# 160 gathered tokens instead of 192, second-table groups of 8 blocks, and x normalised once: one step of a hybrid decoder with product-key experts

## The chip, the cores and the metric

The kernel runs on one core of one Trainium2 chip. The metric is the device time of one execution in microseconds (us). A time of a kernel is the median of several executions; a profile is of one execution more, with a time of its own.

## The reference

One decoder layer for 512 prompt tokens and 8 x 4 sample tokens, 544 in all, of width 2048. A combined projection, a gated MLP and an RWKV-7 recurrence make the hidden state `h`; none of that is touched. What follows is the expert part:

```
def peer_ffn(xn, ...):                        # xn = rms_norm(h) * norm2_g
    q = xn @ w_q                              # 8 heads, 2 halves of 128
    s = q . sub_keys                          # 128 scores per head and half
    top 16 of each half -> 256 sums -> top 16 experts, gates = softmax of their scores
    act = gelu(u_tab[expert] . xn)            # 16384 experts, a row of 2048 each
    out = sum over 8 * 16 experts of gate * act * v_tab[expert]
y = rms_norm(h + out) * final_g
```

All is float32. Each token thus needs 128 rows of `u_tab` and 128 rows of `v_tab`, two tables of 134 MB each.

## The kernel before

`front` computes the projection, the two head groups and part of the output projection. `back` (from line 610) does the rest, and the diff touches it alone. Matrix products are split in three: a weight tile is loaded (`wr`), rounded to a short form on ScalarE (`wh`, line 661) and its remainder is taken on VectorE (`wl`, line 662); the product is `wh*xh + wh*xl + wl*xh`. Each table tile holds 1024 columns of 128 and serves 24 matmuls.

The expert part treats the tokens in two ways. The first `TD` = 352 tokens use **whole tables**: for each of 128 blocks of 128 experts, `activations` (line 763) multiplies the block of `u_tab` with all 352 tokens (48 matmuls, line 675), and `products` (line 1062) multiplies blocks of `v_tab` with the coefficients (line 1071). The coefficients are the Gelu of the first times `G`, a table of gates that is zero where a token has not chosen an expert. `G` is built in groups of `GT` = 32 tokens (`NG` = 11 groups, lines 1016 to 1032) and stored in HBM (`Gd`). The last `TG` = 192 tokens use **gathers**: waves of 32 tokens, each with 64 steps in which GpSimd's indirect DMA (line 807) fetches 128 rows of 8 KB and VectorE makes one pass over them, a dot product with x for `u_tab` (line 819) or a weighted sum for `v_tab` (line 838). `ROWS` = 3 buffers hold the rows. `finish` sums a wave's results with a few matmuls (line 862), adds h, normalises and stores.

Order of the stages in `back`: the output projection's second half, with h, its square sum and x = h times `norm2_g` (not yet divided by the norm; `xh`, `xl` for the first 416 tokens, `th`, `tl` for the last 128, whose queries come out transposed); the query product with the top-k of the last two token tiles beside it; then the top-k and `decode` of the other three tiles, each step with one `early` first-table block beside it, whose activations go to HBM (`Cd`); then `G`, with an early block per group; then the main loop over 128 blocks. 52 early blocks, the odd ones 1 to 103, are done before the main loop. There each is loaded from `Cd`, the others are computed. For every block GpSimd multiplies by `G` (line 1055, from `gl`, loaded for four blocks at a time), ScalarE rounds the coefficients to `ch` (line 1058) and GpSimd takes the remainder `cl` (line 1059). After each `GB` = 4 blocks come 8 calls of `products`. Each fills two PSUM tiles of 12 matmuls; six tiles exist. VectorE adds each tile to `y` (line 1079), which is `last`. `cc` has `GB + 2` = 6 slots for `ch` and `cl`.

Because x is not yet divided by its norm, every first-table block is multiplied by `rs2` on VectorE as it leaves PSUM (line 768); the Gelu follows on ScalarE (line 769). `last` is the multiplication, and `gathers` makes the next fetch and the next pass wait for it:

```python
        work[0] += n if steps else 0
        while nstep[0] < min(STEPS, int(work[0])):
            ...
            steps[0].send(after)
```

A step is due at fixed places: one per early block, and in the main loop `PACE * left` steps are spread with weight 6 on a computed first-table block and 4 on a call of `products`, 1480 in all.

Engines run their instructions in order. Within an engine the order comes from a scheduler with priorities: table splits are drawn ahead (by 300 in the main loop, 1500 before it), the eviction of a block by 60. Queues: SP issues all loads, GpSimd the stores to HBM and the gathers.

Of the kernel before, what the change touches and what calls it, by code (L numbers as in the profile page):

```python
# [11 lines left out]
OP = mybir.AluOpType  # L12
# [575 lines left out]

TG = 192
TD = TC - TG  # L590
# [7 lines left out]
GT = 32  # L598
GB = 4
STEPS = (64 + ROWS - 1) * NW  # L600
# [9 lines left out]
def back(tc, I, O, SC):  # L610
# [35 lines left out]
    res = pool(es, "res")  # L646
    bv = res.tile([128, ntile, 8, 16], F32, name="bv")
    e1 = res.tile([128, ntile, 8, 16], F32, name="e1")
    e2 = res.tile([128, ntile, 8, 16], F32, name="e2")
    idx = [res.tile([128, 32], U32, name=f"idx{w}") for w in range(NW)]  # L650
# [36 lines left out]

    rsp = pool(es, "rsp")
    rs2 = rsp.tile([128, TC], F32, name="rs2")
    ms = rsp.tile([TT, 1], F32, name="ms")  # L690
    with ExitStack() as s1:
# [4 lines left out]
        yp = pool(s1, "yp")  # L696
        xh = x2.tile([128, KT, TQ], F32R, name="xh2")
        xl = x2.tile([128, KT, TQ], F32R, name="xl2")
        xt = pool(xts, "xt", side="right")
# [60 lines left out]

    cp = pool(es, "cp", 3)
# [25 lines left out]
    gp, rows, po = [], [], []  # L787

    def gather_steps(w):
        c = WAVES[w]  # L790
        t, r0 = divmod(c, 128)
        rw = slice(r0, r0 + 32)
        xrow, acc = rows
        ef = gp[0].tile([128, 128], F32, name="ef")
        V.scalar_tensor_tensor(ef[rw], f2(e1[rw, t]), 128.0, f2(e2[rw, t]), op0=OP.mult, op1=OP.add)
        for j in range(4):
            js = slice(j * 32, j * 32 + 32)
            V.tensor_copy(idx[w][js], ef[rw, js])
            V.tensor_copy(gts[w][js], f2(bv[rw, t])[:, js])
        msw = gp[0].tile([128, 1], F32, name="msw", bufs=2)  # L800
# [88 lines left out]
    def open_gathers():  # L889
# [4 lines left out]
        next(steps[0])  # L894

    with ExitStack() as s1:
        tk = pool(s1, "tk", 2)
# [58 lines left out]
        for h in range(8):  # L956
# [34 lines left out]
            topk(sc[:, 1], 4, h)  # L991
            topk(sc[:, 0], 3, h)
        early(3)
        decode(4)
        decode(3)
        open_gathers()
        for t in range(3):
            for h in range(8):
                early(1)
                topk(sc0[:, h, t], t, h)  # L1000
            early(ED)
            decode(t)


    NG = TD // GT
    NE = -(-TD // 128)
    with ExitStack() as s1:
# [24 lines left out]
        early(EARLY)  # L1032


    yp = pool(es, "y")
    yT = yp.tile([128, KT, TD], F32, name="y")
    with ExitStack() as s1:
        vp = pool(s1, "vp")
        cc = pool(s1, "cc", GB + 2)
        po.append(pool(s1, "po", 6, space=PSUM))  # L1040
        r4 = lambda t: t.rearrange("p (g t) -> p g t", t=GT)
        NGR = 128 // GB
        gl, cs, ss = {}, {}, []

        def coefficients(b):
            g, i = divmod(b, GB)
            if i == 0:
                gl[g] = vp.tile([128, NG, GB, GT], F32, name="gl", bufs=2)
                S.dma_start(gl[g], SC["G"][:, :, b:b + GB].rearrange("g p b t -> p g b t"))
# [5 lines left out]
            G.tensor_mul(r4(ac), r4(ac), gl[g][:, :, i])  # L1055
            ch = cc.tile([128, TD], F32R, name="ch")
            cl = cc.tile([128, TD], F32R, name="cl")
            A.copy(ch, ac)
            G.tensor_sub(cl, ac, ch)  # L1059
            cs[b] = ch, cl  # L1060

        def products(g, m2):
            ws = split(wp, I["vT"][g, m2], 300)
            ps = [po[0].tile([128, 512], F32, name="o") for j in range(2)]
            for i0, i1 in ((0, GB - 1), (GB - 1, GB)):
                for j in range(2):
                    for i in range(i0, i1):
                        hi, lo = (w[:, (j * GB + i) * 128:(j * GB + i) * 128 + 128] for w in ws)
                        ch, cl = cs[g * GB + i]
                        for n, (a, x_) in enumerate(((hi, ch), (hi, cl), (lo, ch))):  # L1070
                            T.matmul(ps[j][:, :TD], a, x_, start=i + n == 0,  # L1071
                                     stop=i == GB - 1 and n == 2)
            for j in range(2):
                m = 2 * m2 + j
                prev = yT[:, m]
                if g == 0:
                    prev = vp.tile([128, TD], F32, name="hr")
                    S.dma_start(prev, SC["hT"][m][:, :TD])
                last = V.tensor_add(yT[:, m], ps[j][:, :TD], prev)  # L1079
                if g == NGR - 1:  # L1080
                    if m == 0:
                        A.activation(ss[0], yT[:, m], AF.Square)
                    else:
                        sq = cp.tile([128, TD], F32, name="ac")
                        A.activation(sq, yT[:, m], AF.Square)
                        G.tensor_add(ss[0], ss[0], sq)
                    A.activation(yT[:, m], yT[:, m], AF.Copy, scale=P("fg", m))
            return last


        left = STEPS - work[0]
        total = VW * 8 * NGR + UW * (128 - EARLY)
        for b in range(128 + 1):
            if b == 128:
                ss.append(vp.tile([128, TD], F32, name="hr"))
            if b < 128:
                coefficients(b)
                if b > GB and b not in firsts:
                    gathers(PACE * left * UW / total, last)
            if b and b % GB == 0:  # L1100
                for m2 in range(KT // 2):
                    last = products(b // GB - 1, m2)
# [50 lines left out]
def layout(inp):  # L1153
# [11 lines left out]
    for n in ("w0", "a0", "k_k", "k_a", "r_k", "gn_g", "gn_b"):  # L1165
# [27 lines left out]
    out["vT"] = np.ascontiguousarray(  # L1193
        out["v_tab"].reshape(128 // GB, GB, 128, 8, 2, 128).transpose(0, 3, 2, 4, 1, 5)
    ).reshape(128 // GB, 8, 128, 2 * GB * 128)
    return out
# [27 lines left out]
```

## Time and profile before

| | us |
|---|---|
| median of 3 runs | 4056.84 (4054.25 to 4058.28) |
| the profiled execution | 4046.83 |
| its span, first to last instruction | 4044.7 |
| TensorE / VectorE / ScalarE / GpSimd busy | 3632.6 / 3084.6 / 1425.5 / 1282.9 |

The mean granted clock of TensorE is 0.958 of full speed. The time of an execution is a little longer than its span. Busy shares are of the whole span; matmuls overlap, so a busy TensorE is not one at its peak. The stages lie in this order: `front` to about 1062 us, the output projection to 1285, the query product to 1472, early blocks and top-k to 1866, `G` to about 2043, the main loop to about 4025.

### The profile page before, as it was taken

To read this page: it belongs to the slowest core of one execution; us is meant where nothing else is said; L and a number is where in the kernel's file an instruction comes from. 1 tells how busy PE (TensorE), PEld (TensorE's weight loads), DVE (VectorE), ACT (ScalarE), POOL (GpSimd) and SP (SyncE) were. 2 spreads that over 40 slices of the span, in tenths; PEclk is the share of its full clock that TensorE was granted. 3 is DMA by queue.
4 is the path that set the end of the run, shared out by engine and by line. 5 is a ranking of instruction groups with operands and counts; after the bars stand their busy time and mean duration, and the time that the engine had idled before them with its cause. 6 is when DMAs were issued, how large, how long until landed. Compare 5 with 4: busy or idle time off the path is not lost.

```text
span 4044.7 us, 65633 instructions
## 1 busy us (share of the span) xinstructions
PE 3632.6 (90%) x25519; PEld 3413.5 (84%) x25519; DVE 3084.6 (76%) x5034; ACT 1425.5 (35%) x2501; POOL 1282.9 (32%) x1190
## 2 busy tenths in 40 slices
PE   8999999999999998889988888888988888898997
PEld 8888888887898997889888778887978788888997
DVE  4566666666645579999957888888898888888995
ACT  4244444444333232227942222222222222223233
POOL 1212222222143002221134443444434443444453
PEclk9999999999999999999999989999999998999998
DMA  4211111112554236667677898889889888998983
GB/s 156 102 62 56 58 59 57 59 57 78 178 170 120 75 115 234 235 225 260 252 242 287 311 341 310 318 310 341 317 326 325 317 322 305 333 331 311 358 332 123
DMA packets 252822, 886.53 MB, mean 219 GB/s; under 512 B 26920, under 2 KB 84008, under 8 KB 200480
## 3 DMA queue, kind: packets, MB, share of 16 engines
q1 hardware_dynamic: 184672, 423.77, 31.5%
q0 software_dynamic: 67840, 458.57, 30.3%
q8 instruction: 201, 3.29, 0.3%
q14 instruction: 109, 0.89, 0.1%
HBM read 823.47 MB, written 58.76 MB: 218 GB/s over the span
## 4 chain that ended last, share of the span: by engine, by line
PE 47%; DVE 16%; issue 15%; DMA 12%; POOL 8%; ACT 1%; SPq 0%; DVEq 0%; POOLq 0%; ACTq 0%
PE g L171 10%; PE o L1071 9%; PE g L675 9%; DMA row<-in_v_tab,idx 4%; PE q L970 4%; DVE wl L662 4%; DMA row<-in_u_tab,idx 3%; POOL row L807 3%; PE i L419 2%; DVE row L819 2%; DMA wr<-in_vT 2%; PE g L573 2%; POOL ac L1055 2%; POOL cl L1059 2%; DMA wr<-in_uT 1%
## 5 line engine op out<-in xcount | busy, mean ns | idle before, releaser
L661 ACT CAST wh<-wr 128x1024 fp32r<-128x1024 f32 x560 | 585.7, 1049 | 1441.4 <-PE o L1071 540.5
L662 DVE TENSOR_TENSOR wl<-wr,wh 128x1024 fp32r<-128x1024 f32 x560 | 730.3, 1308 | 205.2 <-ACT wh L661 200.4
L1071 PE MATMUL o<-ch,wh 128*128 128x352 f32 x2048 | 688.3, 343 | 190.1 <-DVE y L1079 146.8
L675 PE MATMUL g<-xh,wh 128*128 128x352 f32 x2048 | 678.3, 331 | 70.0 <-DVE ac L768 59.0
L1071 PE MATMUL o<-cl,wh 128*128 128x352 f32 x2048 | 695.0, 340 | 41.7 <-POOL cl L1059 41.7
L1071 PE MATMUL o<-ch,wl 128*128 128x352 f32 x2048 | 687.2, 337 | 0.7 <-DVE wl L662 0.7
L675 PE MATMUL g<-xh,wl 128*128 128x352 f32 x2048 | 672.9, 329 | 3.5 <-DVE wl L662 3.5
L675 PE MATMUL g<-xl,wh 128*128 128x352 f32 x2048 | 671.8, 328 | 0.0
L1071 PEld LDWEIGHTS o<-ch,wh 128*128 128x128 f32 x2048 | 407.5, 200 | 218.1 <-DVE y L1079 80.5
L819 DVE SCALAR_TENSOR_TENSOR row<-row,xrow 128x2048 f32<-128x2048 f32 x192 | 457.2, 2382 | 92.1 <-DMA row<-in_u_tab,idx 90.8
L838 DVE SCALAR_TENSOR_TENSOR acc<-row,dots,acc 128x2048 f32<-128x2048 f32 x186 | 458.8, 2467 | 63.7 <-DMA row<-in_v_tab,idx 61.6
L807 POOL DMA_INDIRECT row<-in_u_tab,idx x192 | 291.0, 1516 | 618.1 <-DVE y L1079 259.1
L675 PEld LDWEIGHTS g<-xh,wh 128*128 128x128 f32 x2048 | 391.4, 191 | 81.8 <-issue 40.9
L1071 PEld LDWEIGHTS o<-cl,wh 128*128 128x128 f32 x2048 | 411.2, 201 | 49.2 <-POOL cl L1059 49.0
L807 POOL DMA_INDIRECT row<-in_v_tab,idx x192 | 264.7, 1379 | 572.1 <-DVE y L1079 341.6
L1071 PEld LDWEIGHTS o<-ch,wl 128*128 128x128 f32 x2048 | 409.8, 200 | 1.0 <-DVE wl L662 1.0
L675 PEld LDWEIGHTS g<-xh,wl 128*128 128x128 f32 x2048 | 392.0, 191 | 5.6 <-DVE wl L662 5.4
L675 PEld LDWEIGHTS g<-xl,wh 128*128 128x128 f32 x2048 | 393.0, 192 | 1.0 <-issue 1.0
L171 PE MATMUL g<-xh,wh 128*128 128x276 f32 x1248 | 379.3, 304 | 9.6 <-ACT xh L113 9.6
L171 PE MATMUL g<-xl,wh 128*128 128x276 f32 x1248 | 375.9, 301 | 0.2 <-DVE xl L114 0.2
L171 PE MATMUL g<-xh,wl 128*128 128x276 f32 x1248 | 374.6, 300 | 0.0
L1079 DVE TENSOR_TENSOR y<-o,y 128x352 f32<-128x352 f32 x496 | 238.7, 513 | 36.0 <-PE o L1071 36.0
(636 smaller groups left out, 6378.6 us busy)
## 6 DMA issues: line engine op xcount, KB each, us to landing
wr<-in_uT SPq DMA_DIRECT2D x256, 512.0 KB
wr<-in_vT SPq DMA_DIRECT2D x256, 512.0 KB
wr<-in_w_in SPq DMA_DIRECT2D x172, 256.0 KB
Gd<-st POOLq DMA_DIRECT2D x11, 2048.0 KB
gl<-Gd SPq DMA_DIRECT2D x32, 704.0 KB
wr<-in_w_q SPq DMA_DIRECT2D x32, 512.0 KB
Cd<-ac POOLq DMA_DIRECT2D x52, 176.0 KB
ac<-Cd SPq DMA_DIRECT2D x52, 176.0 KB
```

The lines of the kernel that those rows point to most:

```text
L171: T.matmul(ps[:M, :HC], a, b[:, k, c], start=n == 0, stop=n == 3 * KT - 1)
L419: return halves(lambda o, c, h: T.matmul(o, a[hs[h], c], b[hs[h], c], start=True, stop=True))
L573: T.matmul(ps[:, :TC // 2], a, b[:, k, h * TC // 2:(h + 1) * TC // 2], start=n == 0, stop=n == 23)
L661: A.copy(hi, raw)
L662: V.tensor_sub(lo, raw, hi)
L675: T.matmul(ps[:, :N], a, b[:, k, c], start=n == 0, stop=n == 3 * KT - 1)
L807: d = G.indirect_dma_start(out=u, out_offset=None, in_=tab, in_offset=bass.IndirectOffsetOnAxis(ap=idx[w][:, r:r + 1], axis=0))
L819: i = V.scalar_tensor_tensor(u, u, 1.0, xrow, op0=OP.mult, op1=OP.mult, accum_out=dots[w][:, r:r + 1])
L838: i = V.scalar_tensor_tensor(acc, u, dots[w][:, r:r + 1], acc, op0=OP.mult, op1=OP.add)
L970: T.matmul(ps[c][:, :TQ], w[:, j:j + 128], x, **e)
L1071: T.matmul(ps[j][:, :TD], a, x_, start=i + n == 0, stop=i == GB - 1 and n == 2)
L1079: last = V.tensor_add(yT[:, m], ps[j][:, :TD], prev)
```

## The change

- `TG` 192 -> 160, so `TD` 352 -> 384: five gather waves instead of six, 384 columns for the whole tables, 12 groups of `G`.
- `GB` 4 -> 8. `products` takes one 128-row piece of the output (`m`) with 8 blocks, 24 matmuls into one PSUM tile, instead of two pieces with 4 blocks each; `vT` is laid out for it. `gl` is still loaded for 4 blocks (`GL`). `ch`/`cl` have 8 slots in `cc` and a ninth behind x.
- The queries' x and the first table's x share one buffer, `xx`. After the query product h is loaded again, multiplied by `norm2_g` and `rs2`, and split into `xh`, `xl` for 384 tokens. `activations` then evicts by the Gelu alone, and `last` is the Gelu.
- The gathers' indices and gates are made right after `decode` (`expert_rows`), the gates' copies on ScalarE; the top-k results and `rs2` are freed before the main loop.

```diff
-TG = 192
+TG = 160
-GB = 4
+GB = 8
+GL = 4
...
+        xx = x2.tile([128, 2 * KT * TQ], F32R, name="xx")
+        def parts(n):
+            return (xx[:, i * KT * n:(i + 1) * KT * n].rearrange("p (k t) -> p k t", t=n)
+                    for i in range(2))
+        xh, xl = parts(TQ)
...
         with tc.high_priority(offset=UP):
-            last = V.tensor_mul(ac, ps, rs2[:, :TD])
-            A.activation(ac, ac, AF.Gelu)
+            last = A.activation(ac, ps, AF.Gelu)
...
+    def expert_rows(t):
+        for w, c in enumerate(WAVES):
+            if c // 128 != t:
+                continue
+            rw = slice(c % 128, c % 128 + 32)
+            ef = tkr.tile([128, 128], F32, name="ef")
+            V.scalar_tensor_tensor(ef[rw], f2(e1[rw, t]), 128.0, f2(e2[rw, t]), op0=OP.mult, op1=OP.add)
+            for j in range(4):
+                js = slice(j * 32, j * 32 + 32)
+                V.tensor_copy(idx[w][js], ef[rw, js])
+                A.copy(gts[w][js], f2(bv[rw, t])[:, js])
...
+        xh, xl = parts(TD)
+        for m in range(KT):
+            r = cp.tile([128, TD], F32, name="ac")
+            S.dma_start(r, SC["hT"][m][:, :TD])
+            V.scalar_tensor_tensor(r, r, P("n2g", m), rs2[:, :TD], op0=OP.mult, op1=OP.mult)
+            A.copy(xh[:, m], r)
+            V.tensor_sub(xl[:, m], r, xh[:, m])
         early(3)
-        decode(4)
-        decode(3)
+        for t in (4, 3):
+            decode(t)
+            expert_rows(t)
...
+    s2.close()
+    s3.close()
...
-        cc = pool(s1, "cc", GB + 2)
+        cc = pool(s1, "cc", GB)
...
+            if b % (GB + 1) == GB:
+                o = 2 * KT * TD
+                ch, cl = xx[:, o:o + TD], xx[:, o + TD:o + 2 * TD]
+            else:
+                ch = cc.tile([128, TD], F32R, name="ch")
+                cl = cc.tile([128, TD], F32R, name="cl")
...
-        def products(g, m2):
-            ws = split(wp, I["vT"][g, m2], 300)
-            ps = [po[0].tile([128, 512], F32, name="o") for j in range(2)]
-            for i0, i1 in ((0, GB - 1), (GB - 1, GB)):
...
+        def products(g, m):
+            hi, lo = split(wp, I["vT"][g, m], 300)
+            ps = po[0].tile([128, 512], F32, name="o")
+            for i in range(GB):
+                ch, cl = cs[g * GB + i]
+                b = slice(i * 128, i * 128 + 128)
+                for n, (a, x_) in enumerate(((hi, ch), (hi, cl), (lo, ch))):
+                    T.matmul(ps[:, :TD], a[:, b], x_, start=i + n == 0, stop=i == GB - 1 and n == 2)
```

## Rows read from the trace of the kernel before

**Rows 1.** The page's first part: busy us of each engine, its share, instructions.

```profile
PE 3632.6 (90%) x25519; PEld 3413.5 (84%) x25519; DVE 3084.6 (76%) x5034; ACT 1425.5 (35%) x2501; POOL 1282.9 (32%) x1190
```

**Rows 2.** Windows by stage: stretch, its length, busy us, PEclk, DMA share, GB/s.

```profile
1472.00:1866.00 394.00, 333.03 (x2005) 325.19 (x2004) 386.65 (x970) 127.12 (x165) 92.63 (x75) 0.95 0.68 228
1866.00:2043.00 177.00, 171.34 (x1183) 161.46 (x1183) 159.97 (x250) 170.00 (x452) 23.66 (x28) 0.99 0.68 246
2089.50:3609.40 1519.90, 1295.58 (x7426) 1250.02 (x7426) 1264.31 (x1196) 408.44 (x485) 641.97 (x476) 0.93 0.88 317
3609.40:4024.50 415.10, 386.18 (x2273) 374.71 (x2271) 337.20 (x328) 138.69 (x176) 187.74 (x126) 0.95 0.80 291
```

**Rows 3.** Windows: one stretch of the second table, then one of the first.

```profile
2805.80:2850.70 44.90, 33.47 (x194) 32.92 (x194) 35.35 (x28) 10.25 (x13) 21.85 (x16) 0.89 0.86 313
2850.70:2865.90 15.20, 15.20 (x97) 15.20 (x97) 14.45 (x15) 4.61 (x5) 4.29 (x5) 1.00 0.97 358
```

**Rows 4.** Groups by line, TensorE, 2089.5 to 3609.4: count, mean, idle before.

```profile
L1071 PE MATMUL o<-cl,wh 128*128 128x352 f32 x1664 | 567.2, 341 | 33.1 <-POOL cl L1059 33.1
...
L1071 PE MATMUL o<-ch,wh 128*128 128x352 f32 x1664 | 560.2, 345 | 180.1 <-DVE y L1079 145.4 <-DVE row L863 17.8 <-ACT ch L1058 12.1
L675 PE MATMUL g<-xh,wh 128*128 128x352 f32 x801 | 260.0, 325 | 9.0 <-ACT wh L661 9.0
```

**Rows 5.** Waits of TensorE in that stretch: us in total, times, longest.

```profile
PE o L1071 <- DVE y L1079: 145.4, 50, 9.7
PE o L1071 <- POOL cl L1059: 33.1, 19, 4.8
PE o L1071 <- DVE row L863: 17.8, 4, 7.8
PE o L1071 <- ACT ch L1058: 12.1, 8, 5.5
```

**Rows 6.** Chain that ended last, in order of time: start, us, what.

```profile
190.90 43.85 PE g L171 x345
...
3609.52 30.51 PE g L675 x192
```

**Rows 7.** Timeline of TensorE inside the query product: start, us, instruction.

```profile
1331.15 0.54 PE L970 MATMUL q<-xl,wh 128*128 128x416 f32 x2
1331.52 0.28 PE L972 MATMUL qt<-wh,tl 128*128 128x256 f32 x1
```

**Rows 8.** Groups by line, VectorE, 2089.5 to 3609.4.

```profile
L662 DVE TENSOR_TENSOR wl<-wr,wh 128x1024 fp32r<-128x1024 f32 x309 | 409.5, 1331 | 97.3 <-ACT wh L661 93.1 <-PE o L1071 3.6
L838 DVE SCALAR_TENSOR_TENSOR acc<-row,dots,acc 128x2048 f32<-128x2048 f32 x138 | 344.0, 2493 | 53.3 <-DMA row<-in_v_tab,idx 52.8
L819 DVE SCALAR_TENSOR_TENSOR row<-row,xrow 128x2048 f32<-128x2048 f32 x128 | 308.1, 2408 | 71.6 <-DMA row<-in_u_tab,idx 70.5
L1079 DVE TENSOR_TENSOR y<-o,y 128x352 f32<-128x352 f32 x394 | 189.3, 512 | 14.5 <-PE o L1071 14.5
L768 DVE TENSOR_TENSOR ac<-g,rs 128x352 f32<-128x352 f32 x51 | 26.2, 514 | 4.9 <-PE g L675 4.9
```

**Rows 9.** Groups by line, GpSimd, 2089.5 to 3609.4.

```profile
L807 POOL DMA_INDIRECT row<-in_v_tab,idx x142 | 182.3, 1284 | 394.9 <-DVE y L1079 296.5 <-DVE acc L838 59.7 <-DMA row<-in_v_tab,idx 21.7
...
L1055 POOL TENSOR_TENSOR ac<-ac,gl 128x352 f32<-128x352 f32 x101 | 144.8, 1437 | 133.2 <-ACT ac L769 80.3 <-DMA ac<-Cd 52.0
L1059 POOL TENSOR_TENSOR cl<-ac,ch 128x352 fp32r<-128x352 f32 x101 | 131.8, 1310 | 22.0 <-ACT ch L1058 20.9
```

**Rows 10.** Windows around the decoding of the first two token tiles.

```profile
1505.00:1520.00 15.00, 15.00 (x96) 15.00 (x95) 15.00 (x25) 6.89 (x9) 0.65 (x1) 1.00 0.52 159
1520.00:1535.00 15.00, 3.41 (x18) 3.15 (x17) 14.80 (x33) 1.54 (x2) 0.43 (x1) 0.72 0.22 74
```

**Rows 11.** Timeline of GpSimd: the first and the last of 11 stores.

```profile
1877.34 0.56 POOL L1030 DMA_DIRECT2D Gd<-st  x1 [3.31 <-ACT st L1029]
...
2048.28 0.56 POOL L1030 DMA_DIRECT2D Gd<-st  x1
```

**Rows 12.** Groups by line, VectorE, 1850 to 2060: a wave's indices and gates.

```profile
L798 DVE CAST idx<-ef 32x32 uint32<-32x32 f32 x20 | 3.5, 173 | 0.3
L799 DVE COPY gt<-bv 32x32 f32<-32x32 f32 x20 | 3.4, 169 | 0.2
```

More of the change, by code (lines that the diff above doesn't have):

```diff
@@ L646, in back @@
     res = pool(es, "res")
-    bv = res.tile([128, ntile, 8, 16], F32, name="bv")
-    e1 = res.tile([128, ntile, 8, 16], F32, name="e1")
-    e2 = res.tile([128, ntile, 8, 16], F32, name="e2")
     idx = [res.tile([128, 32], U32, name=f"idx{w}") for w in range(NW)]
@@ L686, in back @@
     pg = pool(pgs, "pg2", 2, space=PSUM)
-    rsp = pool(es, "rsp")
+    cp = pool(es, "cp", 3)
+    s3 = ExitStack()
+    rsp = pool(s3, "rsp")
     rs2 = rsp.tile([128, TC], F32, name="rs2")
@@ L787, in back @@
     gp, rows, po = [], [], []
+    def expert_rows(t):
[9 more added lines that the diff above has]
+                A.copy(gts[w][js], f2(bv[rw, t])[:, js])
     def gather_steps(w):
         c = WAVES[w]
-        t, r0 = divmod(c, 128)
-        rw = slice(r0, r0 + 32)
         xrow, acc = rows
[L794 to L799, printed above, removed]
         msw = gp[0].tile([128, 1], F32, name="msw", bufs=2)
@@ L894, in open_gathers @@
         next(steps[0])
+    s2 = ExitStack()
+    tkr = pool(s2, "tkr")
+    bv, e1, e2 = (tkr.tile([128, ntile, 8, 16], F32, name=n) for n in ("bv", "e1", "e2"))
     with ExitStack() as s1:
@@ L1002, in back @@
             decode(t)
+            expert_rows(t)
     NG = TD // GT
@@ L1046, in coefficients @@
             g, i = divmod(b, GB)
-            if i == 0:
-                gl[g] = vp.tile([128, NG, GB, GT], F32, name="gl", bufs=2)
-                S.dma_start(gl[g], SC["G"][:, :, b:b + GB].rearrange("g p b t -> p g b t"))
+            if b % GL == 0:
+                gl[b // GL] = vp.tile([128, NG, GL, GT], F32, name="gl", bufs=2)
+                S.dma_start(gl[b // GL], SC["G"][:, :, b:b + GL].rearrange("g p b t -> p g b t"))
             if b in firsts:
@@ L1054, in coefficients @@
                 ac, _ = activations(b, 300)
-            G.tensor_mul(r4(ac), r4(ac), gl[g][:, :, i])
-            ch = cc.tile([128, TD], F32R, name="ch")
-            cl = cc.tile([128, TD], F32R, name="cl")
+            G.tensor_mul(r4(ac), r4(ac), gl[b // GL][:, :, b % GL])
+            if b % (GB + 1) == GB:
[4 more added lines that the diff above has]
+                cl = cc.tile([128, TD], F32R, name="cl")
             A.copy(ch, ac)
@@ L1060, in coefficients @@
             cs[b] = ch, cl
-        def products(g, m2):
-            ws = split(wp, I["vT"][g, m2], 300)
-            ps = [po[0].tile([128, 512], F32, name="o") for j in range(2)]
-            for i0, i1 in ((0, GB - 1), (GB - 1, GB)):
[L1066 to L1087, printed above, removed]
@@ new lines, in products @@
+        def products(g, m):
[6 more added lines that the diff above has]
+                    T.matmul(ps[:, :TD], a[:, b], x_, start=i + n == 0, stop=i == GB - 1 and n == 2)
+            prev = yT[:, m]
+            if g == 0:
+                prev = vp.tile([128, TD], F32, name="hr")
+                S.dma_start(prev, SC["hT"][m][:, :TD])
+            last = V.tensor_add(yT[:, m], ps[:, :TD], prev)
+            if g == NGR - 1:
+                if m == 0:
+                    A.activation(ss[0], yT[:, m], AF.Square)
+                else:
+                    sq = cp.tile([128, TD], F32, name="ac")
+                    A.activation(sq, yT[:, m], AF.Square)
+                    G.tensor_add(ss[0], ss[0], sq)
+                A.activation(yT[:, m], yT[:, m], AF.Copy, scale=P("fg", m))
@@ L1088, in products @@
             return last
         left = STEPS - work[0]
-        total = VW * 8 * NGR + UW * (128 - EARLY)
+        total = VW * KT * NGR + UW * (128 - EARLY)
         for b in range(128 + 1):
@@ L1100, in back @@
             if b and b % GB == 0:
-                for m2 in range(KT // 2):
-                    last = products(b // GB - 1, m2)
+                for m in range(KT):
+                    last = products(b // GB - 1, m)
                     gathers(PACE * left * VW / total, last)
@@ L1193, in layout @@
     out["vT"] = np.ascontiguousarray(
-        out["v_tab"].reshape(128 // GB, GB, 128, 8, 2, 128).transpose(0, 3, 2, 4, 1, 5)
-    ).reshape(128 // GB, 8, 128, 2 * GB * 128)
+        out["v_tab"].reshape(128 // GB, GB, 128, KT, 128).transpose(0, 3, 2, 1, 4)
+    ).reshape(128 // GB, KT, 128, GB * 128)
     return out
```

3 lines of the change are left out of this document (removed).

## The prediction

> **What bounds the kernel now.** I read the busy shares first: TensorE has 90% of the span, VectorE 76% [rows 1]. That is an average over stages with different limits, so I cut the span where the code changes stage. Up to about 1472 us nothing that the diff touches costs anything different. From there four stretches matter [rows 2]: the early first-table blocks beside the top-k (VectorE busy 387 of 394 us: its work is the time there), the building of the coefficient table G (ScalarE 170 and TensorE 171 of 177 us), the two tables while half of the first one's blocks come from the store (1520 us), and the end, where all of them are computed (415 us).
>
> The third stretch is nearly two fifths of the span and no engine fills it: TensorE 1296, VectorE 1264, DMA share 0.88. It alternates between two kinds of work [rows 3]. While the first table is multiplied, TensorE is busy all of 15.2 us at full clock. While the second is, it is busy 33.5 of 44.9 us at a granted clock of 0.89. So first-table work already runs at TensorE's pace, and the loss sits in `products`.
>
> How large is it? 345 matmuls of 276 columns take 43.85 us and 192 of 352 columns 30.51 us [rows 6]: 127.1 and 158.9 ns each, 0.418 ns a column. The stretch has 4992 + 2402 matmuls of 352 columns [rows 4] (each of their three operand pairs has the same count to within one), 1175 us at 158.9 ns. The other 345 us are lost: 224 us idle (the idle times of rows 4 with their small companions), and 121 us of matmuls at the lower of the clock's two levels (1.2 GHz instead of 2.4) and of the gathers' own sums. The waits name the cause: 145 of 224 us are for the add of `y`, which must empty a PSUM tile, and the longest is 9.7 us; 45 us for `ch` and `cl`, 18 us for the gathers' closing adds [rows 5]. VectorE is late with `y` because it works in order: a product pair costs it 1.33 us for `wl`, two adds of 0.51 and nearly one gather pass of 2.45, 4.8 us [rows 8] against 24 x 158.9 ns = 3.8 us on TensorE, and it sits idle 53 + 72 us for rows that have not landed. Six PSUM tiles of 12 matmuls, two being filled, give only four tiles, 7.6 us, of cover.
>
> **The change part by part.** All sums are against the profiled execution: 4046.8 us, of which 4044.7 is the span. The median shown is 10 us above it; I add that at the end.
>
> *More columns.* 32 more tokens go through the tables: 352 becomes 384 columns. By the slope a matmul costs 13.4 ns more, 172.3 ns. From the other side, two matmuls of 416 columns start 0.37 us before the next instruction [rows 7], 185 ns each, and halfway between is 172 ns. The third stretch's 7394 matmuls then need 1274 us (+99), the last one's 2273 need 392 instead of 361 (+31). The early blocks' share, 36 x 48 x 13.4 ns = 23 us, lies under VectorE, which fills that stretch; without that cover it is paid.
>
> *One wave fewer.* Gather steps left for the main loop fall from 396 - 49 = 347 to 330 - 49 = 281, so the stretch's 266 passes become about 215. VectorE is spared 51 x 2.45 = 125 us, the DMA queues 51 x 1.05 MB.
>
> *Groups of 8.* A product now fills one PSUM tile with 24 matmuls instead of two with 12: as many weight splits, half the adds (189 us becomes 189/2 x 384/352 = 103). Six tiles, one being filled, cover 5 x 24 x 172 ns = 20.7 us instead of 7.6. The longest waits, 9.7 and 7.8 us, fit in the 13 us gained. G's loads stay in fours.
>
> *x normalised.* `rs2` leaves the eviction: ScalarE's Gelu reads PSUM itself, and VectorE loses 26 us here [rows 8]. VectorE's load in the stretch becomes 1264 - 125 - 86 - 26 = 1027 us. Bytes: 317 GB/s over 1520 us is 482 MB, less 53, plus 2 for wider G and C, 431 MB; at the present rate of the busy DMA engines (482 MB in 0.88 x 1520 = 1337 us) that is 1195 us. TensorE, at 1274, becomes the largest load. The DMA engines can go higher than 0.88: first-table stretches hold 358 GB/s at a share of 0.97 [rows 3].
>
> The Trainium skill (DMA: Bandwidth & Descriptors, section Bandwidth) states 425 GB/s for one core's 16 MB transfers and about 358 where HBM limits. An estimate from its higher figure would be 431/425 = 1014 us of transfers; the stretch's own rows give 1195, and I use these.
>
> What stays lost? Below: nothing, 1274 us. Above: all 345 us, 1619. I take the `y` wait from 145 to 20 us, nearer the lower end because every one of its 50 instances is shorter than the new cover; the closing adds from 18 to 0; `ch`/`cl` from 45 to 30, since there are half as many boundaries; the other 16 as they are. That is 66 us idle, and the 121 us scaled with the idle time, 36. Sum 1376, or **-144**. In the last stretch `y` hardly waits; of its 54 lost us I keep 40: 432 us, **+17**.
>
> *A tighter ring.* `ch`/`cl` had six slots for groups of four; now nine for eight (the ninth behind x), one spare instead of two. Block 8g+9 can't be written before the group's last product reads block 8g. Its Gelu, GpSimd's product and split then have to fit beside the next first-table blocks: 8 x (1.44 + 1.31) x 384/352 = 24.0 us and about five gather issues of 1.28 [rows 9], 30 us, against four blocks of 8.3 us, 33 us on TensorE. Before it was 14.8 against 15.3. GpSimd waits in order, for rows to come free and for `y`, and behind it stand the next `cl` and then TensorE. I price it inside the 30 us; its other end is a rival.
>
> *The new x.* 16 loads of hT on SP's queue, 16 products and 16 subtractions on VectorE at about 0.51 x 384/352 = 0.56 us, 17.9 us, and 16 casts on ScalarE. `xl` overlies the old x, so its first write waits for the last query matmul, and the first table starts late by up to 18 us. SP's queue is in order, and loads of `uT` may stand behind an hT load that waits for one of three buffers. Against it: 36 multiplications by `rs2` leave VectorE (18.5 us); TensorE sits idle 11.6 us soon after anyway [rows 10]. `expert_rows` makes all five waves' indices there, four more than now, each four casts of 0.17 [rows 12] and one combination; the gates move to idle ScalarE. VectorE comes out even within 3 us. From 0 to 30 us; I take **+8**, nearer to VectorE's even balance.
>
> *G.* 384 tokens are 12 groups instead of 11; the stores lie 170.9 us / 10 = 17.1 us apart [rows 11]: **+17**, and four blocks behind it at TensorE's pace, **+3**.
>
> *At nothing.* Freed top-k tiles and `rs2`: `y`'s new place was last read before the main loop, whose idle start covers it; if not, it is a few us once. A dot or add behind a first-table block now waits for the Gelu instead of for VectorE's own multiplication, and `wl` and `y` stand behind it. ScalarE is busy 408 of 1520 us, so I take 0; the other end is one cast of `wh` ahead of it, about 1 us, in 51 blocks of that stretch, which the 20.7 us of PSUM cover.
>
> Sum: -144 + 17 + 8 + 17 + 3 = -99. 4046.8 - 99 = 3948, and with the 10 us to the median **3958 us**.
>
> **Rivals.** *TensorE never waits.* VectorE at 1027 and DMA at 1195 of 1274 us would speak for it; against it, two streams that both come in bursts. Then -246 in the third stretch, -23 in the last, +20: 3808 at the extreme, some 3860 halfway.
>
> *The lost time stays (slower).* If TensorE waits not for want of PSUM tiles but for gathered rows that land late ahead of `wl` and `y` in VectorE's order, deeper tiles only move the wait, and it shrinks no faster than the passes: 345 x 281/347 = 279, so 1553 (+33), +17, +28: 4135 us. For it: 125 us of VectorE idle on rows. Against it: none of those waits is over 10 us. It decides once more than 201 of the 345 us stay, the 102 that the forecast keeps and the 99 that it gains.
> The Trainium skill (TensorE: Matmul & The Clock Gate, the section on psum-queue depth-cycling) warns that small idles between groups that cycle through PSUM tiles keep the clock swinging. The trace agrees that product stretches have 0.89 where first-table ones have 1.00; by that rule the 121 us would stay whole and the sum come to about 4043.
>
> *The ring is the new wait.* If GpSimd's 30 us start only when VectorE has finished the group's last adds, 10 to 17 us stick out at each of 13 boundaries: 130 to 220 us, beginning to cost the whole gain at 99/13 = 7.6 us each. Halfway, about 4060. Today a boundary costs 45/26 = 1.7 us, which speaks against it.
>
> **How the numbers follow.** Forecast 66%, TensorE without waits 12%, lost time stays 11%, ring 11%. The forecast's own bounds are 3890 to 4030; reaching to parts of the other cases gives 3865 to 4055. Within 0.2% (8 us) of 4056.8 is about what a measurement can tell from no change: 7%, mostly the ring; slower 13%; faster 80%.
>
> **What would show it.** Product stretches near 4.2 to 4.5 us per 24 matmuls with a clock near 1; `y` waits of TensorE below 40 us; 384-column matmuls at 172 ns; G's stores still 17 us apart. I am wrong if `cl` or `ch` heads TensorE's waits, if the first table starts over 20 us late, or if `y` still waits above 100 us.

## Result and the profile after

The changed kernel takes **3997.4 us** (median of 4 runs, 3982.2 to 4005.1) against 4057.6 us (4 runs) for the kernel before beside it. The ratio is **0.9848**, 95% interval [0.9818, 0.9878]; timed again in the third set of experiments it was 0.9848 [0.9808, 0.9887]. That is 60 us faster where 99 were forecast. The profiled execution took 3982.2 us with a span of 3980.1, so between the two profiled executions the gain is 64.6 us, and the accounts below are made against that. (The changed kernel's profiled execution lies 15 us under its median, the one before 10 us under.)

In the page's first part, to be read against [rows 1], VectorE fell by 288 us, and TensorE now fills 95% of a shorter span:

```profile
PE 3769.2 (95%) x25575; PEld 3560.8 (89%) x25575; DVE 2796.1 (70%) x4566; ACT 1442.4 (36%) x2570; POOL 1374.7 (35%) x1126
```

Windows of the changed kernel with the columns of [rows 2]: the two tables while half of the first one's blocks come from the store, the end, then one product stretch and the first-table stretch behind it, as in [rows 3]:

```profile
2117.00:3530.20 1413.20, 1337.18 (x7323) 1308.96 (x7322) 1018.87 (x852) 396.93 (x471) 712.99 (x416) 0.97 0.83 300
3530.20:3958.30 428.10, 412.72 (x2273) 401.89 (x2272) 288.66 (x234) 139.83 (x177) 200.38 (x117) 0.98 0.73 259
...
3015.00:3089.40 74.40, 71.63 (x386) 70.33 (x385) 52.65 (x45) 21.75 (x25) 31.11 (x19) 0.95 0.74 267
3089.40:3122.70 33.30, 33.30 (x194) 33.30 (x193) 24.59 (x19) 8.43 (x11) 20.69 (x12) 1.00 0.94 346
```

The third stretch is 1413 us instead of 1520, but TensorE did 96 fewer first-table matmuls in it: two more blocks were computed ahead of the first product. At 173.5 ns each that is 16.6 us, so the like-for-like gain is 90 us. The stretch's idle time (length less TensorE's busy time) went from 224 to 76 us. A product stretch of 384 matmuls in 74.4 us is 4.65 us per 24, at a clock of 0.95.

Waits of TensorE in that stretch, to be read against [rows 5]. The additions of `y` are gone from the list altogether. What heads it is `ch`, and a new line has come in: first-table matmuls waiting for ScalarE's Gelu (L772), which now empties their PSUM tile.

```profile
PE o L1097 <- ACT ch L1086: 22.9, 15, 8.0
PE g L673 <- ACT ac L772: 18.4, 8, 5.4
PE o L1097 <- POOL cl L1087: 13.6, 22, 3.3
PE g L673 <- DVE wl L660: 11.4, 4, 6.9
PE o L1097 <- DVE wl L660: 6.3, 4, 2.1
```

The chain that ended last has unbroken rows like those of [rows 6]: 935 and 144 first-table matmuls of 384 columns at 175.3 and 175.0 ns each, 384 products at 176.4.

```profile
1512.76 163.94 PE g L673 x935
...
2239.98 67.73 PE o L1097 x384
2311.26 25.20 PE g L673 x144
```

VectorE's groups in the stretch, against [rows 8]: 213 gather passes instead of 266, half as many additions of `y` at 553 ns instead of 512. The waits for rows that have not landed are still there, 86 and 78 us, beside 151 us for ScalarE's casts `wh`:

```profile
L660 DVE TENSOR_TENSOR wl<-wr,wh 128x1024 fp32r<-128x1024 f32 x305 | 405.7, 1335 | 150.9 <-ACT wh L659 150.9
L846 DVE SCALAR_TENSOR_TENSOR acc<-row,dots,acc 128x2048 f32<-128x2048 f32 x110 | 264.0, 2400 | 88.6 <-DMA row<-in_v_tab,idx 86.3
L827 DVE SCALAR_TENSOR_TENSOR row<-row,xrow 128x2048 f32<-128x2048 f32 x103 | 244.9, 2378 | 79.9 <-DMA row<-in_u_tab,idx 77.7
L1102 DVE TENSOR_TENSOR y<-o,y 128x384 f32<-128x384 f32 x191 | 105.4, 553 | 47.5 <-PE o L1097 46.3
```

Timeline of GpSimd, the first and the last store of G, against [rows 11]. Twelve stores lie in 170.96 us, as long as eleven did before: 15.5 us apart, not 17.1.

```profile
1881.11 0.57 POOL L1052 DMA_DIRECT2D Gd<-st  x1 [15.86 <-ACT Rt L1049]
...
2052.07 0.55 POOL L1052 DMA_DIRECT2D Gd<-st  x1 [0.86 <-ACT st L1051]
```

### The profile page after: what moved, and what is told of

Its sections match the earlier page's. It is cut to its first block, busy times and chain, and to the rows that moved or that the text cites. A ratio compares the mean times of both kernels' runs of the same rounds, so it can differ in the third digit from the quotient of the medians.

```text
span 3980.1 us, 65004 instructions
## 1 busy us (share of the span) xinstructions
PE 3769.2 (95%) x25575; PEld 3560.8 (89%) x25575; DVE 2796.1 (70%) x4566; ACT 1442.4 (36%) x2570; POOL 1374.7 (35%) x1126
## 4 chain that ended last, share of the span: by engine, by line
PE 53%; issue 13%; DMA 11%; POOL 10%; DVE 9%; ACT 3%; SPq 0%; DVEq 0%; POOLq 0%; ACTq 0%
PE o L1097 12%; PE g L673 12%; PE g L171 10%; DMA row<-in_v_tab,idx 4%; POOL row L815 4%; PE q L982 4%; POOL ac L1079 2%; PE i L419 2%; PE g L573 2%; POOL cl L1087 2%; DMA row<-in_u_tab,idx 2%; DVE wl L660 2%; DMA hr<-hT 2%; PE i L171 1%; PE qt L984 1%
## 5 line engine op out<-in xcount | busy, mean ns | idle before, releaser
L673 PE MATMUL g<-xx,wh 128*128 128x384 f32 x4096 | 1076.8, 342 | 37.4 <-ACT ac L772 30.0
L673 PEld LDWEIGHTS g<-xx,wh 128*128 128x128 f32 x4096 | 751.1, 191 | 46.7 <-ACT ac L772 34.5
L673 PE MATMUL g<-xx,wl 128*128 128x384 f32 x2048 | 699.6, 342 | 23.8 <-DVE wl L660 23.7
L1097 PE MATMUL o<-ch,wh 128*128 128x384 f32 x1824 | 629.3, 345 | 22.9 <-ACT ch L1086 22.9
L1097 PE MATMUL o<-cl,wh 128*128 128x384 f32 x1824 | 629.9, 345 | 14.3 <-POOL cl L1087 14.3
L1097 PE MATMUL o<-ch,wl 128*128 128x384 f32 x1824 | 627.0, 344 | 6.3 <-DVE wl L660 6.3
L673 PEld LDWEIGHTS g<-xx,wl 128*128 128x128 f32 x2048 | 392.3, 192 | 29.5 <-DVE wl L660 29.3
L171 PEld LDWEIGHTS g<-xh,wh 128*128 128x128 f32 x1248 | 236.6, 190 | 19.4 <-ACT xh L113 9.7
L1079 POOL TENSOR_TENSOR ac<-ac,gl 128x384 f32<-128x384 f32 x128 | 188.8, 1475 | 178.6 <-DMA ac<-Cd 114.3
L171 PEld LDWEIGHTS g<-xl,wh 128*128 128x128 f32 x1248 | 236.6, 190 | 11.5 <-issue 4.9
```

Source lines behind the costliest of these rows:

```text
L171: T.matmul(ps[:M, :HC], a, b[:, k, c], start=n == 0, stop=n == 3 * KT - 1)
L673: T.matmul(ps[:, :N], a, b[:, k, c], start=n == 0, stop=n == 3 * KT - 1)
L1079: G.tensor_mul(r4(ac), r4(ac), gl[b // GL][:, :, b % GL])
L1097: T.matmul(ps[:, :TD], a[:, b], x_, start=i + n == 0, stop=i == GB - 1 and n == 2)
```

## The experiments

All run beside the kernel before; each time is a median of 5 to 12 runs, and a ratio is to the runs of before in the same set (medians 4058.1, 4056.8 and 4052.5 us). A ratio is not the quotient of the two medians shown, so a gain by the ratio can differ by some us from one by the medians. In the tables that follow, "two tables" is the window from the first product matmul's start to the last one's end, and "idle" that length less TensorE's busy time. "Per 24" is worked out from the trace: the times from each matmul's start to the start of the next, added up by the table that the first of them belongs to, times 24 over the count. These readings are of one profiled execution each, and such an execution can lie far from its kernel's median (f2: 4013.7 against 4036.3 us). `front`, which no edit touches, ends between 1139 and 1167 us in them; the window of the two tables leaves that part out.

### First set: which part carries it

**e1: the eviction back on VectorE.** In the changed kernel:

```
-            last = A.activation(ac, ps, AF.Gelu)
+            last = V.tensor_copy(ac, ps)
+            A.activation(ac, ac, AF.Gelu)
```

> The changed kernel, but a first-table block leaves PSUM by a copy on VectorE, and ScalarE's Gelu works in SBUF, as before the change (x stays normalised). Theory A, the Gelu as eviction is what eats the gain: it stands behind a ch cast that waits for GpSimd and the load from Cd, TensorE's wait for line 772 (20 us in the main loop) and part of the waits for wl and ch go away, 15 to 40 us below the changed kernel, near 3965. Theory B, the nine slots for eight blocks are the new wait: no change, 3990 to 4005, ch and cl still head TensorE's waits. Theory C, VectorE is still short: 51 + 23 copies of 0.5 us more on it, 10 to 30 us slower.

Measured 3990.1 us, 0.9845 [0.9813, 0.9877]: the same as the changed kernel. TensorE's waits between 2050 and 3960 us for the eviction became 39.4 us on VectorE where 20.0 had been on ScalarE. With 160 tokens and groups of 8 the Gelu's move to PSUM neither gains nor costs anything measurable. That is theory B's time, but not its cause: `cl` and `ch` stand at 16.3 and 13.4 us and do not head the waits.

**e2: 192 gathered tokens again**, with groups of 8, the new x and the Gelu eviction (`TG = 192`).

> The changed kernel with 192 gathered tokens again: groups of 8, normalised x and Gelu eviction alone. If the saved gather passes carry the gain, it goes back towards the kernel before, 4030 to 4060. If the groups of 8 carry it, the 352 columns give TensorE back 13.4 ns on 12288 matmuls (some 130 us outside the stages that hide it), VectorE gets 155 us of passes again and the DMA queues 64 MB: 3950 to 4000, at or below the changed kernel, with a DMA share above 0.9 in the main loop.

Measured 4017.9 us, 0.9913 [0.9881, 0.9946]: without the fewer tokens the rest gives 35 us. That lies between the two expectations.

**e3: groups of 4 again**, with 160 tokens, the new x and the Gelu eviction; pairs of 12-matmul products and six slots for `ch` and `cl`, as before the change:

```
-GB = 8
+GB = 4
...
-        cc = pool(s1, "cc", GB)
+        cc = pool(s1, "cc", GB + 2)
...
+            ps = [po[0].tile([128, 512], F32, name="o") for j in range(2)]
+            for i0, i1 in ((0, GB - 1), (GB - 1, GB)):
+                for j in range(2):
```

> The changed kernel with groups of 4 again (two PSUM tiles of 12 matmuls per product call, six ch/cl slots, the old layout of vT): 160 tokens and normalised x alone. If the deeper PSUM cover carries the gain, TensorE waits again for the add of y, about 100 us with its slow matmuls, 4050 to 4110. If the saved passes have already relieved VectorE, the y wait stays below 40 us and the time within 20 us of the changed kernel.

Measured 3979.1 us, 0.9806 [0.9772, 0.984], no slower than the changed kernel. With four tiles of 12 matmuls as cover the wait for `y` has nearly gone all the same; the first lines of TensorE's waits in e3, 2050 to 3960 us (the wait for `y` was 146.8 us before, in the same window):

```profile
PE o L1099 <- POOL cl L1087: 41.1, 26, 7.4
PE o L1099 <- ACT ch L1086: 29.6, 13, 6.6
PE o L1099 <- DVE y L1107: 17.1, 9, 6.1
```

My theory, that the deeper PSUM cover of groups of 8 had removed that wait and brought the gain, fell here.

**e4: the cast of ch on GpSimd**, so that no Gelu and no `wh` stands behind it on ScalarE:

```
-            A.copy(ch, ac)
+            G.tensor_copy(ch, ac)
```

> The changed kernel with the cast to ch on GpSimd instead of ScalarE, so that ScalarE never waits for GpSimd or Cd ahead of a Gelu or a wh cast. Theory A (ScalarE's order): waits of TensorE for line 772 and for wl shrink by some 30 us, and the time by 15 to 40 us, if GpSimd, 50% busy, can take 128 casts of about 1 us. Theory B (the ring and GpSimd's chain): the chain per block grows by 0.5 us or more, and cl waits grow, 10 to 40 us slower.

Measured 3999.3 us, 0.986 [0.9827, 0.9894]: the same. The wait for the Gelu fell from 20.0 to 2.0 us, but those for `ch` rose from 22.9 to 40.5, for `cl` from 14.3 to 19.0 and for the products' `wl` from 6.3 to 14.2. Neither theory's time came about.

### Second set: the other corners, and the load behind ch

**f1: the new x and the Gelu eviction alone** (192 tokens, groups of 4).

> The kernel after with 192 gather rows and groups of 4 blocks (the old product order, six closing slots): against the kernel before only x normalised and split anew, the Gelu as eviction and the freed top-k results are left. Theory 1, the fewer gather tokens carry the change and grouping carries nothing: with 192 tokens and groups of 8 the ratio was 0.991, and groups of 4 give the same, 4010 to 4030 us, so that the 0.991 is what the new x and the Gelu eviction bring (the VectorE product out of PSUM is gone). Theory 2, groups of 8 carry the 0.991 at 192 tokens, where VectorE's queue is full and the wait for the y additions long: without them 4050 to 4065 us, with waits of TensorE for y near the 145 us of before. Reading: time, and the waits for y between 2050 and 3960 us.

Measured 4057.0 us, 1.0003 [0.9976, 1.003]: nothing, and the additions of `y` still hold TensorE 115 us. So it was the groups that gained in e2, as theory 2 has it.

**f2: groups of 8 with the new x** (192 tokens, eviction on VectorE).

> The kernel after with 192 gather rows and the eviction on VectorE (a copy out of PSUM, Gelu afterwards in SBUF): against the kernel before groups of 8 and the normalised x. Theory 1 (grouping carries nothing, VectorE's 512 ns evictions and PSUM waits at 192 tokens do): 4045 to 4060 us. Theory 2 (groups of 8 carry it): 4010 to 4030 us, as with the Gelu eviction, because at 160 tokens the eviction's engine made no difference. Reading: time, and TensorE's waits for y, ch and cl.

Measured 4036.3 us, 0.9961 [0.9939, 0.9984]: a gain of 16 us by the ratio, 20 by the medians, between the two expectations. The trace shows where the rest went. Here are TensorE's waits, 2050 to 3960 us, of f2:

```profile
PE g L673 <- DVE ac L772: 92.9, 30, 8.4
PE o L1098 <- POOL cl L1088: 39.6, 27, 5.8
...
PE o L1098 <- DVE y L1103: 4.0, 3, 1.5
```

The cover did what it should: `y` waits 4 us instead of 147. But TensorE then reaches the next first-table blocks, which have two PSUM tiles only, while VectorE is still behind, and waits there 93 us for the copy that empties them (14 us for the multiplication in that place before). Per 24, products went from 5.15 to 4.60 us and first-table matmuls from 4.22 to 4.92.

**f3: 160 tokens with the new x** (groups of 4, eviction on VectorE).

> The kernel after with groups of 4 and the eviction on VectorE: against the kernel before only 160 tokens and the normalised x. Theory 1, the fewer gather tokens carry the change: 3975 to 4000 us, y waits under 30 us. Theory 2, the Gelu eviction frees VectorE and matters once groups of 4 need their y additions soon: 4010 to 4040 us, y waits of 60 us and more.

Measured 3978.7 us, 0.983 [0.9794, 0.9866]. Theory 1: the tokens do it, whichever engine empties the PSUM tile.

**f4: four buffers of their own for the activations loaded back**, with groups of 4 and 160 tokens, where the room allows it:

```
-                ac = cp.tile([128, TD], F32, name="ac")
+                ac = vp.tile([128, TD], F32, name="cd", bufs=4)
                 S.dma_start(ac, SC["C"][firsts.index(b)])
```

> The kernel after with groups of 4, and four buffers of their own for the activations that are loaded back (they shared three with the blocks computed in place, so that a load waited for the third block before it). Theory 1, GpSimd's wait for that load holds the casts and through ScalarE's order the Gelu evictions and weight casts: GpSimd's wait for the load, 147 us with groups of 4, falls under 30, TensorE's waits for cl and ch (41 and 30 us) by half or more, and the time by 25 to 45 us to 3935 to 3955. Theory 2, that wait lies beside other waits (the paced gathers' wait for the y additions, 465 us on GpSimd, comes in its place): TensorE's waits for cl and ch stay within 15 us and the time at 3970 to 3990 us.

Measured 3984.7 us, 0.982 [0.9785, 0.9855], as without them. GpSimd's wait for that load fell from 147 us in e3 to 31, but a wait of 111.5 us for the load of G's rows, which the same product needs, came up; TensorE's waits for `cl` and `ch` did fall, from 71 to 24 us, and the one for `y` rose from 17 to 62. Theory 2's time, by another wait than the one it named.

```profile
PE o L1099 <- DVE y L1107: 62.2, 24, 5.7
PE o L1099 <- POOL cl L1087: 19.9, 15, 4.3
```

The corners side by side (all but the first line with the new x; a star marks the runs with 96 fewer first-table matmuls in the window, 16.6 us at the changed kernel's pace):

```
tokens, groups, eviction   ratio    two tables  idle   per 24: products, first table
192, 4, VectorE (before)   1        1935.0      253    5.15  4.22
192, 4, Gelu    (f1)       1.0003   1930.8      255    5.16  4.17
192, 8, VectorE (f2)       0.9961   1875.7*     217    4.60  4.92
192, 8, Gelu    (e2)       0.9913   1872.3*     211    4.67  4.77
160, 4, VectorE (f3)       0.983    1849.2       98    4.75  4.34
160, 4, Gelu    (e3)       0.9806   1841.7       95    4.72  4.34
160, 8, VectorE (e1)       0.9845   1835.0*      93    4.57  4.68
160, 8, Gelu    (after)    0.9848   1841.3*      91    4.64  4.61
```

Idle time follows the tokens: about 95 us with 160, whatever the groups, and 211 to 255 with 192. Groups of 8 speed up the products in every pair and slow the first table in every pair. At 192 tokens that exchange leaves 16 to 35 us by the ratios, at 160 no gain that shows.

### Third set: what the fewer tokens are worth, and through what

These three are the kernel before, with 352 columns, in which every fifth gather step is thinned: 72 of 384, about as many in the main loop as the change takes away. In g1 and g3 the row is not fetched:

```
-            queue.append((fetch(I["u_tab" if r < 32 else "v_tab"], r % 32, after), r))
+            queue.append((None if r % 5 == 4 else fetch(I["u_tab" if r < 32 else "v_tab"], r % 32, after), r))
```

In g1 and g2 `work_on` leaves the pass out; in g3 it runs it on the row that is next in line, or on `xrow`:

```
+            if r % 5 == 4:
+                return
```

```
+            if u is None:
+                u = queue[0][0] if r < 32 else xrow
```

**g1: neither row nor pass.**

> The kernel before, with one gather step in five empty: neither the row is fetched nor the pass over it run (72 of 384; about as many as the wave that the change takes away, with 352 columns as before; the sums of the gather rows lack these terms). It prices the fewer passes alone. Theory 1, passes and rows are what TensorE waits behind through the y additions: 160 tokens gained 70 to 80 us net although their wider matmuls cost some 130 us in the two last stretches, so that the passes alone are worth about 200: 3840 to 3880 us, y waits under 40 us. Theory 2, the gain of 160 tokens came from elsewhere (the new order of the early stage): no more than 80 us, 3980 to 4020.

**g2: the pass left out, the row still fetched.**

> The kernel before, with one gather pass in five left out on VectorE while its row is still fetched (the sums lack these terms). Theory 1, VectorE's time decides (the y additions stand behind passes): nearly the whole gain of the run with neither, within 40 us of it. Theory 2, the rows' landing decides (VectorE sat idle 53 and 72 us for rows): less than a third of that gain, 3990 to 4050 us.

**g3: the row left out, the pass still run.**

> The kernel before, with one row in five not fetched while VectorE's pass is still run, on a row that is there (the sums hold other terms in their place). Theory 1 (VectorE's time): within 30 us of before, 4025 to 4057. Theory 2 (the rows' landing and the DMA share of 0.88): at least half of the gain of the run with neither, 3850 to 3960 us, and VectorE's waits for rows nearly gone.

```
                ratio   interval          median us  two tables  idle  VectorE idle for rows
before          1                                    1935.0      253   152
g1, neither     0.9771  [0.9738, 0.9803]  3957.2     1843.5      196   209
g2, no pass     0.9925  [0.9896, 0.9953]  4020.3     1915.2      242   280
g3, no row      1.0001  [0.9976, 1.0026]  4050.6     1928.3      248   130
```

Neither half gives what both give: by the medians 32 us and nothing, against 95. Where only the passes go, VectorE stands waiting for rows instead, 280 us (the sum of its two lines for `row` and `acc`, 2050 to 3960 us; 152 in the kernel before), and the DMA share is 0.90 between 2100 and 3550 us (0.88 before):

```profile
DVE row L821 <- DMA row<-in_u_tab,idx: 164.2, 59, 7.2
DVE acc L842 <- DMA row<-in_v_tab,idx: 116.0, 51, 7.2
```

TensorE's wait for `y` does fall in g2, from 147 to 56 us. But the waits for `ch` and `cl` rise from 61 to 147 us and take most of that back. The first lines, 2050 to 3960 us, of the kernel before and then of g2:

```profile
PE o L1071 <- DVE y L1079: 146.8, 52, 9.7
PE o L1071 <- POOL cl L1059: 41.1, 22, 4.8
PE o L1071 <- ACT ch L1058: 20.0, 11, 5.5
```

```profile
PE o L1075 <- ACT ch L1062: 86.4, 26, 9.9
PE o L1075 <- POOL cl L1063: 60.5, 31, 7.5
PE o L1075 <- DVE y L1083: 55.6, 25, 10.4
```

Where only the rows go, VectorE is as busy as before and TensorE's wait for `y` stays:

```profile
PE o L1075 <- DVE y L1083: 151.1, 59, 9.0
```

But g3 takes away bytes more than waits for rows (130 us against 152): a first-table pass without a row of its own runs on the next row in line, and so waits for that one to land. In time, g2 came out as its theory 2 has it and g3 as its theory 1. The traces show that the passes hold `y` up. That late rows hold it up once the passes are fewer is how g1 (22 us for `y`) reads against g2 (56 us); it is not shown apart from that.

And g1 gained 95 us, between its two expectations and not the 200 that the first rests on. Its waits show the next limit, the casts and subtractions that make `ch` and `cl`, in the same window of TensorE as for e3:

```profile
PE o L1075 <- ACT ch L1062: 89.0, 24, 8.0
PE o L1075 <- POOL cl L1063: 63.4, 26, 9.4
PE o L1075 <- DVE y L1083: 21.7, 11, 9.1
```

Yet 160 tokens with groups of 4 gained 70 to 80 us although their matmuls are wider. Back-to-back matmuls at full clock start 160.6 (products) and 159.3 ns (first table) apart in g1, 174.5 and 173.4 in e3, means of all spacings under 250 ns. With 6144 products and 3504 first-table matmuls in the window of each, that is 1545 us in g1 and 1680 in e3, 135 us more; and the windows are 1843.5 and 1841.7 us long. So the time that is not matmuls at full clock fell from 298 to 162 us: the wider matmuls ran in time in which TensorE had waited or run slowly. This is a comparison of one execution each (f3's window is 1849.2 us) of two kernels that also differ in the early stage and in which rows they leave out; I did not widen the columns alone.

**g4: the changed kernel again.**

> The changed kernel itself, timed again beside the same runs of before, for a closer ratio: its first had 0.9848 with an interval from 0.982 to 0.988, and 160 tokens with groups of 4 had 0.981 and 0.983. If groups of 8 cost something at 160 tokens the ratio is 0.985 to 0.990; if they are indifferent, 0.980 to 0.984.

Measured 3988.6 us, 0.9848 [0.9808, 0.9887], between the two ranges. The interval overlaps those of e3 and f3. The medians lean towards groups of 4 (3979 to 3985 us in e3, f3 and f4, 3989 to 3997 for the changed kernel and e1), but that groups of 8 cost something at 160 tokens is not shown, and no version that computes the whole result is shown to beat the changed kernel.

## Why the prediction came out as it did

The direction and the range were right, the gain was about two thirds of the forecast (64.6 of 99 us between the profiled executions, 60 between the medians), and the step that was to carry it was not the one that did. That the range held is in part luck: two errors of opposite sign, named below, met in the sum.

**The third stretch** was to give 144 us and gave 90. By back-to-back spacings at full clock, its 4992 + 2402 matmuls cost 1187 us before (160.8 and 159.9 ns) and 1296 after (176.1 and 173.5): +109, not +99. The slope taken from 276 and 352 columns was sound for the first table (+13.6 for 13.4 ns); products gained 15.3. The lost time fell from 333 to 134 us, 199 instead of the forecast 345 to 102. These are the two mis-sized terms of the third stretch, 10 and 44 us. Of the 134 us, 76 are idle (66 forecast) and 58 are lost otherwise (36): I had scaled the second part down with the idle time, and it shrank less.

**The failed step** is "Groups of 8", with the reasoning that six tiles with 20.7 us of cover take the `y` wait from 145 to 20 us. The wait did go to nothing in the changed kernel, and f2 shows that the cover alone removes it. But removing it that way gained 16 to 35 us, because the backlog was met elsewhere: at the first table's two PSUM tiles (93 us in f2, 63 for ScalarE's Gelu in e2) and in waits for `wl` (57 us in e2). And with 160 tokens the wait goes without it (17 us in e3, 11 in f3). What carries the gain is the wave that is gone, row and pass together. The columns' cost, which I added in full (+99 and +31) and set against the cover, is largely absorbed by waits that the fewer passes alone leave, as far as g1 and e3 can be compared. The two errors offset each other in the sum; the forecast of VectorE (1027 for 1019 us measured) and of the bytes (431 MB for 300 GB/s over 1413 us, 424 MB) was close and proved nothing about the cause. Of the prediction's own signs, the pace of the products (4.65 us per 24 at a clock of 0.95), of the matmuls (176.1 and 173.5 ns) and of G's stores (15.5 us) missed by little; `y` below 40 us held. One figure beside the forecast is a slip: half way from 3958 to the extreme of 3808 us is 3883, not 3860.

**The rival "lost time stays"** lost on time but named a mechanism that is real: that deeper tiles only move the wait. f2 is that case, with idle time from 253 to 217 us. Its other half, a clock that stays low because TensorE keeps pausing between PSUM tiles, for which the rule of the Trainium skill (TensorE: Matmul & The Clock Gate, the section on psum-queue depth-cycling) was cited, did not come about: the granted clock of the stretch rose from 0.93 to 0.97 as the idle time fell. In the six kernels of the first two sets with 160 tokens it is 0.97 or 0.98 over the two tables, and in every kernel with 352 columns it is 0.93 or 0.94, g1 too.

**The ring of nine slots** is no wait: in the stretch no cast to `ch` and no subtraction to `cl` is released by TensorE giving a slot back. The casts wait 295 us for GpSimd's product by `G`, which waits 109 us for loads from `Cd`. `ch` and `cl` together, with the ninth slot, hold TensorE 40 us (30 forecast, 45 before). By the letter of my own sign I was wrong, as `ch` heads the list; its 23 us show that the sign was badly chosen, since something must head a short list.

**Gelu as eviction, costed at nothing,** has that net price with 160 tokens (e1). But its bound of about 1 us, one cast ahead, was wrong: a single wait is 5.4 us. Here are the timelines of ScalarE, GpSimd and TensorE in the changed kernel (start, length, and in brackets the idle time before and its releaser). TensorE ends a block at 2881.2 us and the one behind it at 2889.5. The next needs the PSUM tile of the first of these, whose Gelu starts only at 2894.35:

```profile
2892.99 0.51 ACT L1086 CAST ch<-ac 128x384 fp32r<-128x384 f32 x1 [9.41 <-POOL ac L1079]
2893.40 1.04 ACT L659 CAST wh<-wr 128x1024 fp32r<-128x1024 f32 x1
2894.35 0.48 ACT L772 ACTIVATE ac<-g 128x384 f32<-128x384 f32 x1
```

```profile
2891.96 0.99 POOL L1079 TENSOR_TENSOR ac<-ac,gl 128x384 f32<-128x384 f32 x1 [7.45 <-DMA ac<-Cd]
```

```profile
2880.87 0.33 PE L673 MATMUL g<-xx,wl 128*128 128x384 f32 x1
...
2888.84 0.51 PE L673 MATMUL g<-xx,wh 128*128 128x384 f32 x2
...
2894.88 1.01 PE L673 MATMUL g<-xx,wh 128*128 128x384 f32 x2 [5.36 <-ACT ac L772]
```

The cast of `ch` stood ahead of it in ScalarE's order and waited for GpSimd, which waited for a load, and a ScalarE busy 28% of the stretch was late. Behind the pause the pair of matmuls takes 1.01 us instead of 0.51, the lower of the clock's two levels. e4 and f4 each take a link out of this chain and gain nothing; in both traces other waits of TensorE grew in its place.

**The front.** The start of the products slipped by 27.5 us, of which 16.6 are the two blocks that moved ahead of it: 10.9 against the forecast 8 + 17 + 3. Of these, 3.7 lie ahead of the new x, where the prediction let nothing change. From `front`'s last matmul to the last query matmul it is 337.3 us (1139.3 to 1476.6) instead of 329.3 (1143.6 to 1472.9), and in every run with the new x 336 to 337 against 330 in g1 to g3. In the changed kernel TensorE is idle for 4.2 of the 25 us from 1130 us on, in the kernel before for none of them; which part of the change does it stays open. From the last query matmul to G's first store it is 404.5 us, 404.4 before: the new x, forecast at 8, cost nothing there, although TensorE waits 7.4 us for it. G cost nothing either, because its stores came 15.5 us apart: there I took a spacing as fixed that had slack in it. The other 7.1 us lie between G's last store and the first product (3 forecast). The last stretch cost 13 us (17 forecast).

So 54 us were missing in the third stretch; 4 in the last stretch and 17 in the front came back, and the kernel's end took 1.5: some 34 us, the difference between 99 and 64.6.

## What to carry to other kernels

Before crediting a deeper buffer with a wait that it covers, look where the late engine meets the same work next: it is the late engine's load that has to fall, and a wait removed without that comes back at the next shallow buffer. Wider work on the engine that waits was nearly free here, where other engines set the pace, so price it against the lost time of the same stretch, not on top of it. And when an engine with little to do is handed an eviction, ask what stands ahead of it in its order and for whom that waits, not how busy it is.

## What the runs showed that was not expected

- Products and first-table matmuls of the same 384 columns don't keep the same pace: 176.1 and 173.5 ns between starts at full clock in the changed kernel, 174.5 and 173.4 with groups of 4. At 352 columns it is 160.8 and 159.9 before, and groups of 8 do not slow the products there (160.5 in f2). Why they add 1.6 ns at 384 is open.
- GpSimd's issue of one row gather, between 2120 and 3930 us, takes 1.33 us (second table) in the kernel before, 1.71 with 192 tokens and groups of 8, 1.82 with 160 and groups of 4 (e3), and 2.14 in the changed kernel. Such spans are rough, and no run was made to find the cause; GpSimd's chain is longer by it than the 1.28 us of [rows 9] that the prediction took. The Trainium skill (SBUF — State Buffer, section on its two separate sides) states that some copies on VectorE lock GpSimd out of a port that it needs to write the descriptors of its own DMAs. No run here tests that, since the profile does not mark such copies. VectorE's work as a whole does not explain the issues: the longest stand where VectorE is busy least (1308 of 1841 us of the two tables in the changed kernel, 1602 of 1935 before).
- Leaving out a fifth of the rows, and with them a DMA share that falls from 0.88 to 0.81 between 2100 and 3550 us, changed nothing in the time (g3).
